# Input projection of a hybrid decoder layer: the first group's P and GB columns as a pair by seven products

## The chip, the cores and the metric

The kernel runs on one core of one Trainium2 chip, as a single launch. The metric is the device time of the launch in microseconds (us). Times of the kernel before are 1523.72, 1524.24 and 1524.89 us in three runs; the median is 1524.24 us. One further execution was profiled; that one took 1524.25 us.

## The reference, cut to what matters

One layer is computed for 256 tokens of width 2048, in float32. Two token mixers share one input projection, whose columns are split into queries, keys, values, a gate z, two small rows, the input of a pooling mixer and two gates:

```python
proj = jnp.einsum('bsd,de->bse', rmsnorm(x, norm_mix_w[l]), w_in[l])
q, k, v, z, b_raw, a_raw, p_in, g_a, g_b = jnp.split(proj, splits, axis=-1)
qkv = jax.nn.silu(causal_dwconv(jnp.concatenate([q, k, v], axis=-1), conv_qkv_w[l]))
...
o = gated_delta_rule(q, k, v, g_log, beta).astype(x.dtype)
y_a = (rmsnorm(o, gdn_norm_w[l]) * jax.nn.silu(z)).reshape(bsz, seq, D_LIN)
pooled = causal_multiscale_pool(p_in.reshape(bsz, seq, N_POOL_GROUPS, POOL_GROUP_DIM))
y_b = jnp.einsum('bsgc,gcd->bsgd', pooled, pool_w[l]).reshape(bsz, seq, D_POOL) * pool_scale[l]
mixed = jax.nn.sigmoid(g_a) * y_a + jax.nn.sigmoid(g_b) * y_b
x = x + jnp.einsum('bsd,df->bsf', mixed, w_out[l])
```

A gated MLP with a causal convolution and a final norm follow. The pooling mixer has four groups of 512 columns, and a group of four heads of the delta rule is as wide; so the kernel works the input projection off in four groups.

## The kernel before, in words

**Tiles and passes.** A weight tile has 256 rows (two blocks of 128) and 512 columns, 512 KB in float32. It is loaded into a buffer `raw` (four in turn), cast by ScalarE (L357) to a rounded float32 `whi`, and VectorE subtracts that from `raw` to get the rest, `wlo` (L368); both have three buffers. The tokens are kept as a high and a low part too. `gemm_a` multiplies a tile with the 256 tokens, in two halves of 128: for each of two blocks and two halves one matmul of high by `whi` (L416), one of low by `whi` (L417), one of high by `wlo` (L418). That makes 12 matmuls of 128x512 for a tile. A block of 2048x512 of the projection is eight tiles, summed in two banks of PSUM, one for each half of the tokens.

**Order of the work.** Group g takes the column blocks K, Q, V, P (the pooling input), GB (the pooling gate), Z, pool and GA, eight tiles each but pool. `srcs` lists the tiles in the order in which they are taken; `weights()` begins the cast and the subtraction of a tile some two tiles ahead. What belongs to the delta rule, the convolutions and the small products is written as a generator (`gdn`, `conv_silu`, `v_conv` and others), of which `side()` runs one piece after each tile. Actions gathered in `later` run when a block's tile number `flush` begins. A scheduler then sets each engine's order of instructions; each engine works its own list strictly in turn.

**Pairs by seven products.** For K and Q of groups 1 to 3, for the output projection and for the MLP, two tiles of each of two column blocks are done together: eight products of a 256x512 tile with half of the tokens (6 matmuls each) become seven, T1, 11, T2, 21, T3, 22 and T4, with sums of weights (`up_sum`, L284, one 128x1024 subtraction each) and sums of tokens. The four tiles, called quads, lie in buffers of their own, each a homes' tag. `pair_product` issues a product and, behind some, puts results together: the result of T1 is copied by ScalarE to `own` in SBUF; that of 11 is copied from one bank into the other (L440); behind T2, VectorE writes `u` = bank + own to SBUF (L443), and at 21 ScalarE copies `u` into the second pair of banks (L432); behind T3, VectorE writes bank + own straight into the second pair (L445). T3 adds to the bank that `u` was read from, so T3's first matmul follows `u`. In the order of K and Q, two items stand between T2 and T3: tile 7 of the block before, and 21.

**What runs in group 0 beside V and P.** The convolutions of K and Q (L931 on ScalarE starts a column block `cy`, then three shifted multiply-adds each on VectorE, L934), the eight exponentials `dec` on ScalarE (L982), whose input row `crow` comes by a DMA and is masked by GpSimd (L974), the eviction of V (`ev`, L876), the value convolution (`vt`, `mv`, L897, L911, L912), then the Gram products (L993, L995) with their diagonals on VectorE (L998). From them a block goes through DRAM to `lb` (`cdd`, L1030, and L1033), and after a wait of so many `side()` calls (`LATE[g]` is part of it) a chain of small VectorE steps on `tb` (L1057 and L1059) inverts 32x32 blocks. The result goes through DRAM again (`tbd`, L1064, to `TT`, L1067), is transposed (L1079), and small matmuls follow (L1103, L1110, then L1121, which reads `U`, copied by ScalarE at L1106, then L1131 and L1139).

Of the kernel before, what the change touches and what calls it, by code (L numbers as in the profile page):

```python
# [28 lines left out]
NR = P // B0  # L29
AHEAD = 2  # L30
WAIT = 5
LATE = (26, 24, 22, 18)
NEVER = -1e30


# [1 line left out]
def kernel(  # L37
# [45 lines left out]
    KQ_FIRST = ("T1", 5, "11", 6, "T2", 7)  # L83
    KQ_MIDDLE = ("21", "T3", "22")
    KQ_THEN = (2, "T4", 3, 4, 5, 6, 7)
    up_w = {("kq", g): [cols(w_in[0], base + 512 * g, KD) for base in (C_K, C_Q)] for g in range(1, 4)}
    srcs = []
    for g in range(4):
        for base in (C_K, C_Q, C_V, C_P, C_GB):
            tiles = cols(w_in[0], base + 512 * g, KD)  # L90
            if g and base == C_K:
                srcs += [("up", ("kq", g), step, 0) if isinstance(step, str) else tiles[step]
                         for step in KQ_MIDDLE + KQ_THEN]
            else:
                srcs += tiles[2:] if g and base == C_Q else tiles
            if g == 0 and base == C_K:
                srcs += [w_in[0, c * 1024 : (c + 1) * 1024, C_B : C_B + P].rearrange("(k p) f -> p k f", p=P)
                         for c in range(2)]
        parts = [cols(pool_w[0, g], 0, 4), cols(w_in[0], C_Z + 512 * g, KD)]
        for part in parts if g == 3 else parts[::-1]:  # L100
            srcs += part
        tiles = cols(w_in[0], C_GA + 512 * g, KD)
        srcs += tiles[:5]
        pair = ("kq", g + 1) if g < 3 else ("out", 0)
        srcs += [("up", pair, step, 0) if isinstance(step, str) else tiles[step] for step in KQ_FIRST]
# [160 lines left out]
    def quad_load(c, n):  # L266

        ch, i = n // 4, (1, 0, 3, 2)[n % 4]
        if c == OUT:
            home = (big if i < 2 else fp).tile([P, 2, 512], F32, tag=OUT_HOMES[i], name=nm("quad"))  # L270
        elif isinstance(c, tuple):
            home = mp.tile([P, 2, 512], F32, tag=KQ_HOMES[i], name=nm("quad"))
        else:
            home = fp.tile([P, 2, 512], F32, tag=UP_HOMES[1 - c % 2][ch][i], name=nm("quad"))
        up_quarters[c, ch, i] = home
        with tc.issue_after(last_load[0]):
            last_load[0] = nc.sync.dma_start(up_quarters[c, ch, i], up_w[c][i % 2][2 * ch + i // 2]).ins
# [105 lines left out]
    def side():  # L383
        next(side_work[0], None)
# [37 lines left out]
    def pair_product(bank, what, tokens, sums):  # L422

        a, b = bank["ps"]
        if what in ("11", "21", "T4"):
            j, t = {"11": (0, 0), "21": (1, 0), "T4": (1, 1)}[what]
            high, low = (lambda kk, f=f: f(2 * j + kk, t) for f in tokens)
        else:
            n = {"T1": 0, "T2": 1, "T3": 2, "22": 3}[what]
            high, low = (lambda kk, s=s: s[:, n, kk * P : (kk + 1) * P] for s in sums)  # L430
        if what == "21":
            nc.scalar.copy(b[:, 0], bank["u"])  # L432
        w = weights()
        ps = {"T1": a[:, 0], "21": a[:, 0], "22": b and b[:, 0]}.get(what, a[:, 1])
        high_first([(ps, high, low)], w, what in ("T1", "11"))
        if what == "T1":
            bank["own"] = cpool.tile([P, 512], F32, tag="sqj", name=nm("own"))
            nc.scalar.copy(bank["own"], a[:, 0])
        elif what == "11":
            nc.scalar.copy(a[:, 0], a[:, 1])  # L440
        elif what == "T2":
            bank["u"] = mp.tile([P, 512], F32, tag="dec0", name=nm("u"))
            nc.vector.tensor_tensor(bank["u"], a[:, 1], bank["own"], op=ALU.add)  # L443
        elif what == "T3":
            nc.vector.tensor_tensor(b[:, 1], a[:, 1], bank["own"], op=ALU.add)  # L445

# [787 lines left out]
    pair_bank = {}  # L1234
    mixing = []

    def kq_steps(steps, ps, flush=3):

        for step in steps:
            if isinstance(step, str):  # L1240
                pair_product(pair_bank, step, (xh, xl), xsums)
            else:
                gemm_a(xh, xl, KD, (step,), ps, flush)

    for g in range(4):
# [27 lines left out]
        if g == 0:  # L1273
# [3 lines left out]
                    fixed_parts()  # L1277

            later.append(after_k)
        e = evict(gemm_a(xh, xl, KD), rsh)  # L1280
        nc.sync.dma_start(vrow[g, SH : SH + S, :].rearrange("(t p) d -> p t d", p=P), e)
        later.append(lambda e=e, g=g, vt2=vt2: v_moved(e, g, vt2))


        win = WINDOWS[g]
        psb = scales(g)
        ps = gemm_a(xh, xl, KD)
        e = evict(ps) if g == 3 else evict(ps, rsh)
        phi = mtile(g, [P, 4, S], F32R, nm("phi"))
        plo = []  # L1290
# [45 lines left out]
                nc.scalar.activation(th[:, t, :], ps[:, t, :], AF.Tanh, scale=rsh[:, t : t + 1])  # L1336
            return th

        tb = gate(gemm_a(xh, xl, KD), "th")
        yb = mp.tile([P, 2, 512], F32, tag="yb", name=nm("yb"))  # L1340
        nc.vector.scalar_tensor_tensor(yb, tb, 1.0, psb.unsqueeze(1).to_broadcast([P, 2, 512]),
                                       op0=ALU.add, op1=ALU.mult)
# [625 lines left out]
```

## Time and profile before

| | |
|---|---|
| median of three runs | 1524.24 us (1523.72 to 1524.89) |
| profiled execution | 1524.25 us, its span 1522.5 us |
| granted TensorE clock | 0.999 |
| first matmul of V, P, GB, Z and GA of group 0 | 60.08, 84.42, 108.82, 134.15, 161.35 us |
| first product of the pair of K and Q of group 1 | 174.95 us |
| DMA | 313.62 MB, mean 206 GB/s |

Times inside the profile count from the start of the span; what lies around the span is the difference of 1.75 us. PE is TensorE's matmuls, PEld its weight loads, DVE is VectorE, ACT is ScalarE, POOL is GpSimd, SP issues most DMAs. In a timeline row stand the start, the length (of a run of like instructions, from the first's start to the last's end), the engine, the line, the operation, what is written and read by tile names, and the shape; a bracket tells of the idle time of the engine before the row and what ended it. Successive instructions of an engine overlap a little, so the step from start to start is shorter than the length.

### The profile page before, as it was taken

Reading aid. Unit: us, or ns where it says so; the run is one execution under the profiler, and the core shown is the slowest. Engines: PE = TensorE matmul, PEld = TensorE weight load, DVE = VectorE, ACT = ScalarE, POOL = GpSimd, SP = SyncE. Lnnn points to the kernel's source line nnn. Section 1 sums busy time; section 2 is a strip of 40 time slices with the busy share of each in tenths; the row PEclk is TensorE's granted clock in tenths of the full one; section 3 lists DMA queues with packets and bytes.
Section 4 is the critical chain, followed back from the end, with each engine's and each line's share of the span. In section 5 each row is a group of like instructions: output and inputs, shape, how many; then the busy total and the mean of one; then the engine's idle time right before and its main releaser. Section 6 shows DMA issues by size and latency. Waiting matters only on the chain.

```text
span 1522.5 us, 20282 instructions
## 1 busy us (share of the span) xinstructions
PE 1513.1 (99%) x7260; PEld 1250.8 (82%) x7260; DVE 1287.0 (85%) x1799; ACT 896.1 (59%) x1160; POOL 75.0 (5%) x97
## 2 busy tenths in 40 slices
PE   9999999999999999999999999999999999999998
PEld 8888888888878888888888888888888888888886
DVE  6779868888688878888777999999998886989896
ACT  7456556455646456456465676667666665555562
POOL 1000001000100001000000000000000011010100
PEclk9999999999999999999999999999999999999999
DMA  8777647784677747774678656666457468566662
GB/s 277 209 226 221 207 139 225 235 255 115 198 221 218 227 127 219 214 238 154 217 227 303 198 164 218 221 212 216 152 164 238 142 212 276 172 223 219 220 220 100
DMA packets 170099, 313.62 MB, mean 206 GB/s; under 512 B 23650, under 2 KB 27010, under 8 KB 169870
## 3 DMA queue, kind: packets, MB, share of 16 engines
q1 hardware_dynamic: 160864, 283.17, 59.0%
q0 software_dynamic: 7344, 27.27, 5.5%
q10 hardware_dynamic: 1790, 1.89, 0.4%
q8 instruction: 57, 0.93, 0.2%
q14 instruction: 44, 0.36, 0.1%
HBM read 303.33 MB, written 8.95 MB: 205 GB/s over the span
## 4 chain that ended last, share of the span: by engine, by line
PE 98%; DVE 1%; issue 1%; ACT 0%; POOL 0%; POOLq 0%; DVEq 0%
PE psg L455 28%; PE psm L418 14%; PE psm L416 14%; PE psm L417 14%; PE psm L1644 8%; PE psg L1644 7%; PE psm L455 4%; PE psm L606 1%; PE psm L1712 1%; PE psg L505 1%; PE psg L993 1%; DVE wlo L368 1%; PE psg L995 0%; PE psm L521 0%; PE psg L1139 0%
## 5 line engine op out<-in xcount | busy, mean ns | idle before, releaser
L357 ACT CAST whi<-raw 128x1024 fp32r<-128x1024 f32 x400 | 419.9, 1052 | 311.0 <-PE psm L417 157.9
L368 DVE TENSOR_TENSOR wlo<-raw,whi 128x1024 fp32r<-128x1024 f32 x398 | 484.1, 1220 | 119.3 <-ACT whi L357 113.9
L357 ACT CAST whi<-quad 128x1024 fp32r<-128x1024 f32 x217 | 227.9, 1053 | 167.5 <-PE psg L455 46.2
L368 DVE TENSOR_TENSOR wlo<-quad,whi 128x1024 fp32r<-128x1024 f32 x217 | 263.4, 1220 | 39.9 <-ACT whi L357 34.8
L416 PE MATMUL psm<-whi,xhl 128*128 128x512 f32 x384 | 150.0, 391 | 0.0
L417 PE MATMUL psm<-whi,xhl 128*128 128x512 f32 x384 | 149.9, 390 | 0.0
L418 PE MATMUL psm<-wlo,xhl 128*128 128x512 f32 x384 | 139.0, 393 | 0.0
L455 PE MATMUL psg<-whi,fhl 128*128 128x512 f32 x504 | 127.1, 389 | 0.0
L284 DVE TENSOR_TENSOR quad<-quad,quad 128x1024 f32<-128x1024 f32 x92 | 111.9, 1217 | 0.1
L455 PEld LDWEIGHTS psg<-whi,fhl 128*128 128x128 f32 x504 | 94.6, 188 | 19.7
L416 PEld LDWEIGHTS psm<-whi,xhl 128*128 128x128 f32 x384 | 72.1, 188 | 15.0
L417 PEld LDWEIGHTS psm<-whi,xhl 128*128 128x128 f32 x384 | 72.1, 188 | 14.9
L418 PEld LDWEIGHTS psm<-wlo,xhl 128*128 128x128 f32 x384 | 71.7, 188 | 14.6
L455 PE MATMUL psg<-wlo,fhl 128*128 128x512 f32 x252 | 69.8, 389 | 0.0
L455 PE MATMUL psg<-whi,ups 128*128 128x512 f32 x216 | 58.1, 391 | 0.0
L455 PEld LDWEIGHTS psg<-wlo,fhl 128*128 128x128 f32 x252 | 47.3, 188 | 9.9
L1644 PE MATMUL psm<-whi,hhi 128*128 128x512 f32 (+1 forms) x140 | 54.2, 387 | 0.0
L1644 PE MATMUL psm<-whi,hlo 128*128 128x512 f32 (+1 forms) x140 | 53.7, 386 | 0.0
L1644 PE MATMUL psm<-wlo,hhi 128*128 128x512 f32 (+1 forms) x140 | 50.2, 386 | 0.0
L455 PEld LDWEIGHTS psg<-whi,ups 128*128 128x128 f32 x216 | 40.3, 188 | 8.5 <-issue 0.2
L1644 PE MATMUL psg<-whi,hhi 128*128 128x512 f32 (+1 forms) x120 | 46.4, 387 | 0.0
L1644 PE MATMUL psg<-whi,hlo 128*128 128x512 f32 (+1 forms) x120 | 46.1, 386 | 0.0
(495 smaller groups left out, 3001.2 us busy)
## 6 DMA issues: line engine op xcount, KB each, us to landing
raw<-in_w_in_dram SPq DMA_DIRECT2D x212, 512.0 KB, 4.5
raw<-in_w_up_dram SPq DMA_DIRECT2D x104, 512.0 KB, 4.7
quad<-in_w_up_dram SPq DMA_DIRECT2D x72, 512.0 KB, 5.3
raw<-in_w_down_dram SPq DMA_DIRECT2D x56, 512.0 KB, 5.1
quad<-in_w_down_dram POOLq DMA_DIRECT2D x32, 512.0 KB, 5.4
raw<-in_w_out_dram SPq DMA_DIRECT2D x24, 512.0 KB, 3.7
mv<-vrow SPq DMA_DIRECT2D x12, 512.0 KB, 4.9
quad<-in_w_in_dram SPq DMA_DIRECT2D x12, 512.0 KB, 6.8
```

Source lines behind the costliest of these rows:

```text
L284: nc.vector.tensor_tensor(out_, plus_, minus_, op=ALU.subtract)
L357: last_cast[0] = nc.scalar.copy(hi, raw).ins
L368: last_split[0] = nc.vector.tensor_tensor(lo, raw, hi.bitcast(F32), op=ALU.subtract).ins
L416: mm(ps[:, t, :], lh(k, t), hi[:, kk, :], start=(k == 0), stop=False, **seeded)
L417: mm(ps[:, t, :], ll(k, t), hi[:, kk, :], start=False, stop=False, **seeded)
L418: mm(ps[:, t, :], lh(k, t), lo[:, kk, :], start=False, stop=(k == nk - 1), **seeded)
L455: last_product[0] = mm(ps, lhs(kk), w[n][:, kk], stop=False, skip_group_check=True, start=(first and n == 0 and kk == 0 and lhs is high)).ins
L505: nc.tensor.transpose(pt[:, ff, t * P : (t + 1) * P], src[:, t, f * P : (f + 1) * P], ident)
L606: mm(ps_k0[:, t, :], part(k, t), w[:, kk, :], start=(k == 0 and w is hi and part is xh), stop=(k == KD - 1 and w is lo))
L993: mm(pg0, kq[:, h, 0, 0:P], kq[:, h, :, :], start=True, stop=True)
L1644: mm(ps[:, cs], lhs(kk), part_[:, kk, cs], start=(first and kk == 0 and n == 0), stop=(last and kk == 1 and n == 2), skip_group_check=shared)
L1712: nc.tensor.transpose(out_[f // 2][:, f % 2, t * P : (t + 1) * P], e[:, t, f * P : (f + 1) * P], ident)
```

## The change

The first two tiles of P and the first two of GB, in group 0, become a pair by seven products: 7 x 6 = 42 matmuls where 8 x 6 = 48 were. The products are not done in a row but set singly among the last tiles of V (T1 behind V's tile 4, then 5, 11, 6, T2, 7, T3) and the tiles of P (21, 2, 22, 3, T4, 4 to 7). GB has only tiles 2 to 7 left, in the banks that the pair has begun. `kq_steps` gets an argument by which `side()` runs after each product. The quads' four buffers are those of `mtile` 1, 2, 5 and 6. The second pair of banks is taken only at 22: `u` and a second sum `u2` (behind T3) are written to SBUF, into the buffers `w1` and `w2`, and ScalarE copies both into the banks then. The wait `LATE` ahead of group 0's `tb` goes from 26 to 19.

```diff
-LATE = (26, 24, 22, 18)
+LATE = (19, 24, 22, 18)
...
+    PG_FIRST = ("T1", 5, "11", 6, "T2", 7, "T3")
+    PG_THEN = ("21", 2, "22", 3, "T4", 4, 5, 6, 7)
+    up_w["pg", 0] = [cols(w_in[0], base, KD) for base in (C_P, C_GB)]
...
+            elif g == 0 and base in (C_V, C_P):
+                srcs += tiles[:5] if base == C_V else []
+                srcs += [("up", ("pg", 0), step, 0) if isinstance(step, str) else tiles[step]
+                         for step in (PG_FIRST if base == C_V else PG_THEN)]
...
-    for pair in (("kq", 1), ("kq", 2), ("kq", 3), ("out", 0)):
+    for pair in (("pg", 0), ("kq", 1), ("kq", 2), ("kq", 3), ("out", 0)):
...
+        elif c == ("pg", 0):
+            home = mtile((1, 2, 5, 6)[i], [P, 2, 512], F32, nm("quad"))
...
-        if what == "21":
+        if what == ("22" if "home" in bank else "21"):
+            if b is None:
+                b = bank["ps"][1] = pm()
+                nc.scalar.copy(b[:, 1], bank["u2"])
             nc.scalar.copy(b[:, 0], bank["u"])
...
-            bank["u"] = mp.tile([P, 512], F32, tag="dec0", name=nm("u"))
+            bank["u"] = mp.tile([P, 512], F32, tag=bank.get("home", ("dec0",))[0], name=nm("u"))
             nc.vector.tensor_tensor(bank["u"], a[:, 1], bank["own"], op=ALU.add)
+        elif what == "T3" and "home" in bank:
+            bank["u2"] = mp.tile([P, 512], F32, tag=bank["home"][1], name=nm("u2"))
+            nc.vector.tensor_tensor(bank["u2"], a[:, 1], bank["own"], op=ALU.add)
...
+            ps = gemm_a(xh, xl, KD, range(5))
+            pair_bank.update(ps=[pm(), None], home=("w1", "w2"))
+            kq_steps(PG_FIRST, ps, 1, True)
...
+            ps = pair_bank["ps"][0]
+            kq_steps(PG_THEN, ps, 2, True)
+            other_ps = pair_bank["ps"][1]
+            pair_bank.clear()
...
-        tb = gate(gemm_a(xh, xl, KD), "th")
+        tb = gate(gemm_a(xh, xl, KD) if g else gemm_a(xh, xl, KD, range(2, 8), other_ps, 2), "th")
```

In the whole program TensorE has 6903 matmuls where it had 6909. VectorE has nine instructions more (four sums, three more `wlo`, `u`, `u2`) and ScalarE seven (three casts, four copies); the counts of SP and GpSimd are the same. The lines move: L357 becomes L366 (cast), L368 L377 (`wlo`), L284 L293 (sum), L416 to L418 become L425 to L427, L455 L470 (a product's matmuls), L443 L455 (`u`), L440 L452 (copy of 11), L931 L946 and L934 L949 (convolution), L982 L997 (`dec`), L1103 L1118, L1110 L1125, L1121 L1136.

**ScalarE around `dec`, at the end of V.** Before, the cast behind the eight exponentials (`whi_975`) is that of P's tile 0:

```order
L357 CAST whi_943<-raw_941 128x1024
...
L931 ACTIVATE cy_812<-psg_802,cqw 128x256
L982 ACTIVATE dec_132_827<-crow_829,ncum 128x128
...
L982 ACTIVATE dec_133_828<-crow_829,ncum 128x128
L357 CAST whi_975<-raw_973 128x1024
L931 ACTIVATE cy_812<-psg_802,cqw 128x256
L931 ACTIVATE cy_812<-psg_807,cqw 128x256
L357 CAST whi_1004<-raw_1002 128x1024
```

Of the change, the first cast here (`whi_972`) is that of V's tile 6, `whi_1003` that of T2, `whi_1020` that of V's tile 7, `whi_1051` that of T3 and `whi_1065` that of 21:

```order
L366 CAST whi_972<-raw_970 128x1024
...
L946 ACTIVATE cy_820<-psg_810,cqw 128x256
L450 COPY own_961<-psm_949 128x512
L997 ACTIVATE dec_136_835<-crow_837,ncum 128x128
...
L997 ACTIVATE dec_137_836<-crow_837,ncum 128x128
L366 CAST whi_1003<-quad_690 128x1024
L946 ACTIVATE cy_820<-psg_810,cqw 128x256
L366 CAST whi_1020<-raw_1018 128x1024
L946 ACTIVATE cy_820<-psg_815,cqw 128x256
L452 COPY psm_949<-psm_950 128x512
L366 CAST whi_1051<-quad_710 128x1024
L366 CAST whi_1065<-quad_762 128x1024
```

The exponentials, which stood ahead of the cast of P's first tile, now stand ahead of that of T2, and V's last tile is cast behind it.

**VectorE at the same place.** Before, from the `wlo` of P's tile 0 to that of P's tile 2 (`wlo_1047`):

```order
L368 TENSOR_TENSOR wlo_977<-raw_973,whi_975 128x1024
L934 SCALAR_TENSOR_TENSOR cy_812<-psg_802,cqw,cy_812 128x255
L934 SCALAR_TENSOR_TENSOR cy_812<-psg_807,cqw,cy_812 128x255
L368 TENSOR_TENSOR wlo_1006<-raw_1002,whi_1004 128x1024
...
L934 SCALAR_TENSOR_TENSOR cy_812<-psg_807,cqw,cy_812 128x253
L368 TENSOR_TENSOR wlo_1047<-raw_1043,whi_1045 128x1024
```

Of the change, from the `wlo` of T2 to that of 21 (`wlo_1067`) and of P's tile 2 (`wlo_1087`); L293 makes the sums for T3 and for T4:

```order
L377 TENSOR_TENSOR wlo_1005<-quad_690,whi_1003 128x1024
L293 TENSOR_TENSOR quad_710<-quad_690,quad_710 128x1024
L949 SCALAR_TENSOR_TENSOR cy_820<-psg_810,cqw,cy_820 128x255
L377 TENSOR_TENSOR wlo_1022<-raw_1018,whi_1020 128x1024
...
L377 TENSOR_TENSOR wlo_1053<-quad_710,whi_1051 128x1024
L293 TENSOR_TENSOR quad_690<-quad_762,quad_690 128x1024
L949 SCALAR_TENSOR_TENSOR cy_820<-psg_815,cqw,cy_820 128x254
L949 SCALAR_TENSOR_TENSOR cy_820<-psg_810,cqw,cy_820 128x253
L455 TENSOR_TENSOR u_1062<-psm_950,own_961 128x512
L377 TENSOR_TENSOR wlo_1067<-quad_762,whi_1065 128x1024
L949 SCALAR_TENSOR_TENSOR cy_820<-psg_815,cqw,cy_820 128x253
L377 TENSOR_TENSOR wlo_1087<-raw_1083,whi_1085 128x1024
```

Between the `wlo` of T2 and `u` stand the `wlo` of V's tile 7 and of T3, two sums and five steps of the convolution.

**TensorE at the end of the group.** Before, the first of the delta rule's small products (L1103) stand behind the pair's product 11 (`wlo_1903`) and inside GA's tile 6 (`wlo_1917`):

```order
L455 MATMUL psm_1900<-wlo_1903,xhl_115 128x512 x2
L1103 MATMUL psg_1646<-T,ga_126_821 32x32 x4
...
L1110 MATMUL psg_1670<-qp_1062,sel 128x32
L418 MATMUL psm_1739<-wlo_1917,xhl_116 128x512
```

Of the change they stand behind the pair's product 22 (`wlo_2017`), inside tile 2 of group 1's K (`whi_2027`):

```order
L470 MATMUL psm_2012<-wlo_2017,xs_784 128x512 x2
L425 MATMUL psm_1918<-whi_2027,xhl1a 128x512
L426 MATMUL psm_1918<-whi_2027,xhl1a 128x512
L1118 MATMUL psg_1599<-T,ga_130_829 32x32 x4
...
L1125 MATMUL psg_1623<-qp_1075,sel 128x32
L425 MATMUL psm_1919<-whi_2027,xhl1a 128x512
L426 MATMUL psm_1919<-whi_2027,xhl1a 128x512
L1136 MATMUL psg_1642<-U_1608,TT 32x32 x8
```

They come later by the rest of GA's tile 6, its tile 7 and four products, and between L1125 and L1136 stand two large matmuls.

More of the change, by code (lines that the diff above doesn't have):

```diff
@@ L93 @@
                          for step in KQ_MIDDLE + KQ_THEN]
+            elif g == 0 and base in (C_V, C_P):
+                srcs += tiles[:5] if base == C_V else []
+                srcs += [("up", ("pg", 0), step, 0) if isinstance(step, str) else tiles[step]
+                         for step in (PG_FIRST if base == C_V else PG_THEN)]
             else:
-                srcs += tiles[2:] if g and base == C_Q else tiles
+                srcs += tiles[2:] if g and base == C_Q or g == 0 and base == C_GB else tiles
             if g == 0 and base == C_K:
@@ L1235, with kq_steps @@
     mixing = []
-    def kq_steps(steps, ps, flush=3):
+    def kq_steps(steps, ps, flush=3, with_side=False):
         for step in steps:
@@ L1241, in kq_steps @@
                 pair_product(pair_bank, step, (xh, xl), xsums)
+                if with_side:
+                    side()
             else:
@@ L1279 @@
             later.append(after_k)
-        e = evict(gemm_a(xh, xl, KD), rsh)
+        if g:
+            ps = gemm_a(xh, xl, KD)
+        else:
+            ps = gemm_a(xh, xl, KD, range(5))
+            pair_bank.update(ps=[pm(), None], home=("w1", "w2"))
+            kq_steps(PG_FIRST, ps, 1, True)
+        e = evict(ps, rsh)
         nc.sync.dma_start(vrow[g, SH : SH + S, :].rearrange("(t p) d -> p t d", p=P), e)
@@ L1286 @@
         psb = scales(g)
-        ps = gemm_a(xh, xl, KD)
+        if g:
+            ps = gemm_a(xh, xl, KD)
+        else:
+            ps = pair_bank["ps"][0]
+            kq_steps(PG_THEN, ps, 2, True)
+            other_ps = pair_bank["ps"][1]
+            pair_bank.clear()
         e = evict(ps) if g == 3 else evict(ps, rsh)
```

## The prediction, blind

> **What bounds the kernel now.** I read the profile page first, for the engine that sets the end: its busy times and its chain of work that ended last.
>
> ```profile
> span 1522.5 us, 20282 instructions
> PE 1513.1 (99%) x7260; PEld 1250.8 (82%) x7260; DVE 1287.0 (85%) x1799; ACT 896.1 (59%) x1160; POOL 75.0 (5%) x97
> PE 98%; DVE 1%; issue 1%; ACT 0%; POOL 0%; POOLq 0%; DVEq 0%
> ```
>
> 98% of the chain is TensorE (PE). The second view is that of TensorE's waits, which says how much of the span isn't matmuls in sequence:
>
> ```profile
> PE psm L521 <- POOL ones L511: 1.1, 1, 1.1
> PE psg L455 <- DVE wlo L368: 0.3, 1, 0.3
> PE psm L418 <- DVE wlo L368: 0.2, 1, 0.2
> ```
>
> These 1.6 us are all, and none lies in the first group's V, P or GB. So a matmul less is worth its cadence, and any wait that the change makes is paid in full. The cadence comes from two stretches of the chain, whose columns are start, length and count:
>
> ```profile
> 839.61 6.80 PE psg L455 x30
> 847.77 23.13 PE psg L455 x102
> ```
>
> 6.80 / 30 and 23.13 / 102 are both 0.2267 us for a 128x512 matmul. The third view is the busy time by stretches of 5 us around the change, columns PE, PEld, DVE, ACT, POOL, granted clock, DMA share, GB/s:
>
> ```profile
> 75.00:80.00 5.00, 5.00 (x28) 4.02 (x27) 2.88 (x6) 1.35 (x4) 0.21 (x1) 1.00 0.68 172
> 80.00:85.00 5.00, 5.00 (x26) 4.14 (x25) 1.11 (x1) 4.54 (x12) 1.01 (x2) 1.00 0.37 143
> 85.00:90.00 5.00, 5.00 (x24) 4.11 (x23) 5.00 (x10) 4.00 (x7) 0.00 (x0) 1.00 0.63 122
> 90.00:95.00 5.00, 5.00 (x24) 4.14 (x23) 4.91 (x7) 2.60 (x4) 0.00 (x0) 1.00 0.79 299
> ```
>
> TensorE never waits here, but VectorE (DVE) goes from 2.88 and 1.11 us of 5 to full between 85 and 95 us. That is where the change sets its pair. The timelines of ScalarE (ACT) and VectorE say why; the columns are start, length, and in brackets the idle time before with what ended it:
>
> ```profile
> 77.07 0.48 ACT L931 ACTIVATE cy<-psg,cqw 128x256 f32<-128x256 f32 x1 [0.30 <-PE psg L505]
> 80.46 2.45 ACT L982 ACTIVATE dec<-crow,ncum 128x128 f32<-128x128 f32 x8 [2.92 <-POOL crow L974]
> 82.82 1.04 ACT L357 CAST whi<-raw 128x1024 fp32r<-128x1024 f32 x1
> 84.48 1.04 ACT L357 CAST whi<-raw 128x1024 fp32r<-128x1024 f32 x1
> ...
> 83.89 1.23 DVE L368 TENSOR_TENSOR wlo<-raw,whi 128x1024 fp32r<-128x1024 f32 x1 [4.80 <-ACT whi L357]
> 85.03 0.87 DVE L934 SCALAR_TENSOR_TENSOR cy<-psg,cqw,cy 128x255 f32<-128x255 f32 x2
> 85.82 1.22 DVE L368 TENSOR_TENSOR wlo<-raw,whi 128x1024 fp32r<-128x1024 f32 x1
> 86.95 1.64 DVE L934 SCALAR_TENSOR_TENSOR cy<-psg,cqw,cy 128x254 f32<-128x254 f32 x4
> ...
> 84.19 0.39 PE L418 MATMUL psm<-wlo,xhl 128*128 128x512 f32 x1
> 84.42 0.39 PE L416 MATMUL psm<-whi,xhl 128*128 128x512 f32 x1
> ```
>
> ScalarE stands until 80.46 at the eight exponentials (dec), which need a row from POOL. So no weight is cast until 82.82, VectorE idles 4.80 us, and then it works off what has gathered. TensorE starts P's first tile at 84.42, with about 1 us in hand.
>
> **The change part by part.** *Matmuls.* Eight tile products of 6 become seven: 6 matmuls less, 6 x 0.2267 = -1.36 us, all on the path.
>
> *Interruptions.* In the changed order TensorE passes from weight matmuls to small ones and back 165 times, before 169, so two interruptions fewer. One costs what it adds beside its own matmuls:
>
> ```profile
> 69.14 0.61 PE L418 MATMUL psm<-wlo,xhl1b 128*128 128x512 f32 x2
> 69.69 0.61 PE L815 MATMUL psg<-mid,glog 128*16 128x128 f32 x4
> 70.23 0.50 PE L416 MATMUL psm<-whi,xhl1b 128*128 128x512 f32 x1
> 70.57 0.40 PE L417 MATMUL psm<-whi,xhl1b 128*128 128x512 f32 x1
> ```
>
> 69.69 is 0.10 later than two cadences after 69.14, and 70.57 is 0.11 later than one after 70.23: 0.2 each, -0.4 us together. Bounds: 0 and -0.4.
>
> *VectorE around V's end.* The change adds nine VectorE instructions, and the order puts the late part of them into the full stretch. ScalarE comes first: its eight dec stand ahead of T2's cast, as ahead of P0's before, and POOL's row is no earlier. So T2's whi is cast from 82.82 to 83.86, V's tile 7 after one more cy (0.41) from about 84.1 to 85.2. TensorE's 48 matmuls up to tile 7 of V are as many as before P0 now, so it would want tile 7 at 84.42: 0.8 us late there. VectorE starts at 83.89 with wlo of T2. In its new order follow the sum for T3, one convolution step (L949 in the new numbering), wlo of tile 7, two steps, wlo of T3, the sum for T4, two steps, and then u (L455 there). From start to start a 128x1024 takes 1.13 to 1.14 us (83.89 to 85.03, 85.82 to 86.95), a step 0.4 (0.87 / 2 and 1.64 / 4). u has a row of its own, from a later group, where L443 makes it:
>
> ```profile
> 186.67 0.69 DVE L443 TENSOR_TENSOR u<-psm,own 128x512 f32<-128x512 f32 x1 [0.20 <-PE psm L455]
> ```
>
> 5 x 1.13 + 5 x 0.41 + 0.69 = 8.4, so u ends at 92.3. T3 must wait for it, because its matmuls add to the bank that u reads. Behind tile 7's start stand 22 matmuls ahead of T3 (12 of tile 7, 6 of T2, the 4 of the 21 with whi): 84.42 + 22 x 0.2267 = 89.41. So TensorE waits 2.9 us, the 0.8 at tile 7 contained. Behind u come wlo of 21 (1.13), a step (0.41) and wlo of P2 (1.13), to 95.0; TensorE has 10 matmuls from T3 to P2's first wlo and arrives at 92.3 + 2.27 = 94.6: 0.4 more. wlo for 22 is ready at 95.0 + 1.13 (vt) + 0.69 (u2) + 1.13 = 97.95, where TensorE gets 18 matmuls later at 99.1: no wait. Sum +3.3 us; 2 if the steps come when VectorE has idled less, 4.5 if each semaphore adds some tenths. What else stands behind the waiting matmul on TensorE's queue is tiles of P; who waits for them is the conv and V's eviction, both with time.
>
> The Trainium skill ("VectorE: DVE Perf Modes", section on the TRN2 errata) says that a VectorE operation pays a fixed extra latency each time, exposed between instructions, and gives (N+151)/0.96 ns for an fp32 add, 1.224 us for 1024. The row's duration agrees with that (1.22 and 1.23), its spacing from start to start doesn't (1.13 to 1.14). By the page's figure the chain to u would end 5 x 0.09 = 0.45 later and the forecast would be 0.45 us higher.
>
> *ScalarE, SP and POOL.* Seven more ScalarE instructions, three casts and four copies, fall where it is busy for 12.5 of 20 us (75 to 95); what they delay is in the walk above. SP's count stays: four loads of P and GB tiles become loads of quads, where the DMA share is 0.37 to 0.79. Nothing, unless a load is late; then what the next tile lacks, up to 1 us. POOL's list doesn't change.
>
> *Side work comes later.* The conv's end, the grams and all that follows them move about three tiles back in the program; only the wait ahead of tb is cut, by 7 calls. The first place where that could tell is lb, which goes through DRAM:
>
> ```profile
> 121.81 3.67 SPq L1030 DMA_DIRECT2D cdd<-ga  x8
> 126.63 2.20 SPq L1033 DMA_DIRECT2D lb<-cdd  x4
> 133.95 0.19 DVE L1057 TENSOR_TENSOR tmp<-lb,tb 128x31 f32<-128x31 f32 x1
> 142.31 0.39 PE L416 MATMUL psm<-whi,xhl1b 128*128 128x512 f32 x1
> ```
>
> Before, from the first cdd to VectorE's first use of lb were 12.1 us. In the new order the second half's grams stand in GB's tile 5 instead of 2, some 6 to 8 us later, so lb is there at about 140 to 142, and its first use stands ahead of wlo of Z's tile 3. TensorE wants that wlo at 143.2, four matmuls after the tile's start at 142.31. VectorE will wait, TensorE just not: 0, and up to 1.
>
> *End of the group.* The chain of tb, which ended at 171.4 behind tile 4 of GA, now ends behind wlo of GA's tile 7, and its way through DRAM follows:
>
> ```profile
> 171.19 0.17 DVE L1059 TENSOR_TENSOR tb<-tb,tmp 128x8 f32<-128x8 f32 x1
> 171.39 2.61 SPq L1064 DMA_DIRECT2D tbd<-tb  x4
> 175.38 1.82 SPq L1067 DMA_DIRECT2D TT<-tbd  x4
> DMA to landing us min/median/max: 1.9/1.9/1.9
> 182.63 1.22 DVE L368 TENSOR_TENSOR wlo<-raw,whi 128x1024 fp32r<-128x1024 f32 x1
> 184.19 0.40 PE L416 MATMUL psm<-whi,xhl 128*128 128x512 f32 x1
> 182.14 1.10 ACT L1106 COPY U<-psg 32x128 f32<-32x128 f32 x4
> ```
>
> The fourth TT issues at 176.8 and lands 1.9 later, 7.3 after tb's end. Tile 7's wlo (182.63) ends 0.4 us ahead of the tile's first matmul (184.19); with the last tb step behind it tb ends 0.2 ahead. In the new order 38 matmuls, 8.6 us, lie from there to the first small product (L1118). The transposes and the addition between them end about 8.4 after tb, at 8.2: in time by 0.4. The product behind it (L1136) needs U, four copies of 1.10 us together, and only L1125 and two matmuls stand between: it comes 0.5 us too soon. Before, 18 large matmuls lay there. +0.5; bounds 0 and 2.8 (below).
>
> Sum: -1.36 - 0.4 + 3.3 + 0.5 = +2.0. The profiled execution took 1524.25 us (1522.5 of span and 1.75 around it), the median of three is 1524.24, so the base is the same: 1524.2 + 2.0 = 1526.3 us.
>
> **The rivals.** *A: the waits are hidden.* It does what seven products for eight can do: -1.36 - 0.4, 1522.5 us. For it speaks that pairs of the same kind run later with hardly a wait while VectorE is nearly full:
>
> ```profile
> 180.00:190.00 10.00, 10.00 (x103) 7.93 (x102) 8.78 (x16) 6.15 (x11) 0.00 (x0) 1.00 0.40 119
> 190.00:200.00 10.00, 10.00 (x66) 7.97 (x66) 9.81 (x14) 6.38 (x10) 0.00 (x0) 1.00 0.19 54
> ```
>
> Against it: there two items stand between T2 and T3, and VectorE idles just before u (0.20 in its row); here one tile does, and VectorE has a backlog. It comes true if u is issued by about 89 us, that is, if dec is over some 3 us sooner because POOL's row comes sooner.
>
> The Trainium skill ("Perfetto Trace Analysis", Identifying the Most-Contended Engine) says that the engine to improve first is the most occupied one, judged by stretch where regimes differ, and that TensorE's busy share is no measure of it. For 85 to 95 us the page would name VectorE (9.91 of 10), and so speaks against adding work to it to save matmuls; TensorE's chain of 98% says the opposite for the whole. By that rule alone VectorE's added late work (sums of T3 and T4, u, 2.95 us) would be paid, less what TensorE saves: 1524.2 + 2.95 - 1.76 = 1525.4, within the forecast's own range.
>
> *B: slower by more than the bound.* The tb chain is late at the group's end. It decides as soon as tb ends 0.2 us after TensorE starts tile 7 of GA: from there each tenth is a wait at L1118. tb stands behind wlo of tile 7, which TensorE needs only ten matmuls into the tile, 2.27 us later. If it comes that late, the wait is 2.27 + 0.2 + 8.4 - 8.6 = 2.3 us: 1528.6. For it: VectorE at 8.78 of 10 there, a long chain of dependent little steps, and lb late at its start; against it: tile 7's wlo was early before.
>
> That the matmuls aren't saved can be left out: the order has 6903 where 6909 stood.
>
> **How the numbers follow.** Forecast 0.55 (1526.3, its own range 1524.5 to 1527.8), A 0.25, B 0.20. The range for all reaches from A less half a microsecond to B and a little: 1522.0 to 1529.0. A measurement of this kernel can tell about 0.2%, 3.05 us: faster is below 1521.2, slower above 1527.3. A lies in the middle band but for 0.03; of the forecast 0.07 lies above; B is above. Faster 0.03, same 0.70, slower 0.27.
>
> **What would show it.** Right: TensorE's waits list T3's matmul (L470) on VectorE's u (L455) with about 2 to 3 us near 90 us; tile 7 of V on ScalarE's cast under 1 us; dec still at about 80.5; 0.5 us at L1136. Wrong: no such wait (A), dec much earlier, or the wait at L1118 on the transposes (B). A time under 1521 would mean that something besides these matmuls had been on the path.

## The result, and the profile after

The changed kernel takes 1541.49 us (median of four runs, 1540.60 to 1543.92), the kernel before 1524.03 us beside it (four runs, 1523.72 to 1524.89). The ratio is 1.0117, interval 1.0104 to 1.0129: 17.5 us slower. The forecast was 1526.3 us, its range ended at 1529.0.

The page of the changed kernel, its span, busy times and the engines' shares of the chain:

```profile
span 1540.2 us, 20284 instructions
...
PE 1519.1 (99%) x7254; PEld 1251.7 (81%) x7254; DVE 1293.3 (84%) x1808; ACT 901.7 (59%) x1167; POOL 70.6 (5%) x97
...
PE 86%; DVE 3%; DMA 2%; issue 1%; SPq 0%; ACT 0%; POOL 0%; POOLq 0%; DVEq 0%
```

TensorE is still busy for 99%, and yet its busy time grew by 6 us with six matmuls fewer: part of the loss is slower matmuls. The waits of TensorE, with sum, count and longest:

```profile
PE psg L1118 <- DVE T L1094: 6.4, 2, 5.2
PE psm L427 <- DVE wlo L377: 3.5, 8, 0.6
PE psm L470 <- DVE u L455: 1.4, 1, 1.4
PE psm L536 <- POOL ones L526: 1.1, 1, 1.1
PE psg L520 <- DVE sz L1432: 0.6, 1, 0.6
PE psg L470 <- DVE wlo L377: 0.3, 1, 0.3
```

13.3 us where 1.6 stood. The forecast wait on `u` is there and half as long; the greatest is on the transposes ahead of the delta rule's small products (L1118), once in group 0 and once, with 5.2 us, elsewhere. To see where, the large weight matmuls of two traces are counted from the end of the program, where both have the same ones, and the starts of the same matmul are subtracted. This gives how late a kernel runs at a place, and the places are ones by which all kernels have done the same small products. The columns are kernels, the last two of them experiments told below:

| place, by its time in the trace of before | forecast, running sum | changed kernel | V's multiplications 3 splits later | pair also set earlier |
|---|---|---|---|---|
| 134.2, Z of group 0 starts | +1.5 | +1.7 | +0.9 | -0.5 |
| 250, group 1 | +2.0 | +5.6 | +5.1 | +0.2 |
| 345, group 1 | +2.0 | +5.8 | +5.2 | +0.2 |
| 527, group 2 | +2.0 | +7.3 | +4.7 | +0.3 |
| 697, group 3 | +2.0 | +10.2 | +4.7 | +0.3 |
| 749, behind group 3's small products | +2.0 | +18.0 | +4.7 | +0.3 |
| 1400, the MLP | +2.0 | +17.8 | +4.4 | 0.0 |

V, P and GB of group 0, where the change is, cost in sum about what was forecast. Only 5.6 us are lost by 250, and 12 more fall in groups 1 to 3, whose code the change doesn't touch. First the place of the change, ScalarE, VectorE and TensorE there (a bracket is the idle time ahead and what ended it):

```profile
79.84 2.45 ACT L997 ACTIVATE dec<-crow,ncum 128x128 f32<-128x128 f32 x8 [1.88 <-POOL crow L989]
...
90.90 0.68 DVE L455 TENSOR_TENSOR u<-psm,own 128x512 f32<-128x512 f32 x1
...
91.63 1.20 PE L470 MATMUL psm<-whi,xs 128*128 128x512 f32 x4 [1.37 <-DVE u L455]
```

`dec` is at 79.84 (before 80.46), `u` ends at 91.6 (forecast 92.3), T3 waits 1.4 us. VectorE has no idle time left there:

```profile
85.00:90.00 5.00, 4.98 (x22) 3.61 (x20) 5.00 (x7) 3.81 (x5) 0.00 (x0) 1.00 0.33 83
90.00:95.00 5.00, 3.54 (x15) 2.42 (x14) 5.00 (x8) 3.04 (x5) 0.00 (x0) 1.00 0.34 128
95.00:100.00 5.00, 4.92 (x22) 3.72 (x21) 5.00 (x7) 3.33 (x5) 0.00 (x0) 1.00 0.93 320
```

The rest of what VectorE owes then comes later: the Gram products of group 0 begin at 108.9 instead of 97.8, and the chain of `tb` ends at 185.5 instead of 171.4. VectorE, SP and TensorE at the end of group 0:

```profile
185.32 0.17 DVE L1074 TENSOR_TENSOR tb<-tb,tmp 128x8 f32<-128x8 f32 x1
185.85 2.62 SPq L1079 DMA_DIRECT2D tbd<-tb  x4
191.47 1.82 SPq L1082 DMA_DIRECT2D TT<-tbd  x4
193.26 1.45 DVE L1094 STREAM_TRANSPOSE T<-TT 32x256 f32<-32x256 f32 x3 [1.78 <-DMA TT<-tbd]
194.86 0.69 PE L1118 MATMUL psg<-T,ga 32*32 32x32 f32 x32 [1.24 <-DVE T L1094]
198.07 0.63 PE L425 MATMUL psm<-whi,xhl1a 128*128 128x512 f32 x1
198.49 0.63 PE L426 MATMUL psm<-whi,xhl1a 128*128 128x512 f32 x1
```

TensorE waits 1.24 us, and a little behind it the matmuls start 0.42 us apart instead of 0.23; the granted clock of 195 to 200 is 0.75. The chain of work that ended last has the two landings, start and length:

```profile
187.86 3.46 DMA tbd<-tb
...
192.35 1.91 DMA TT<-tbd
```

The first took 3.5 us where 1.9 was counted on.

In group 2, VectorE of the kernel before:

```profile
441.18 0.29 DVE L998 CUSTOM_DVE_ANT_0 jk<-psg,ident 128x128 f32<-128x128 f32 x1
...
443.28 0.48 DVE L1012 SCALAR_TENSOR_TENSOR ga<-psg,sj,dec 128x256 f32<-128x256 f32 x1
...
445.47 1.23 DVE L911 TENSOR_TENSOR mv<-mv,taps 128x1024 f32<-128x1024 f32 x1 [0.54 <-DMA mv<-vrow]
```

and of the changed one:

```profile
447.71 0.29 DVE L1013 CUSTOM_DVE_ANT_0 jk<-psg,ident 128x128 f32<-128x128 f32 x1
...
453.21 1.23 DVE L926 TENSOR_TENSOR mv<-mv,taps 128x1024 f32<-128x1024 f32 x1 [5.20 <-DMA mv<-vrow]
454.36 0.28 DVE L1013 CUSTOM_DVE_ANT_0 jk<-psg,ident 128x128 f32<-128x128 f32 x1
...
466.41 0.48 DVE L1027 SCALAR_TENSOR_TENSOR ga<-psg,sj,dec 128x256 f32<-128x256 f32 x1
```

This is the core of the case. Before, the Gram diagonals `jk` and the result `ga` came first and V's multiplication `mv` after them, when its row had nearly landed (0.54 us of waiting). Now half of the diagonals stand behind `mv`. VectorE stands 5.20 us for a DMA, with work in its list that could have run (the Gram products of that half had ended by 448.9), and `ga` is 23 us later, of which the kernel's own lateness there is 5 to 7. The list of VectorE's waits says that it happens three times:

```profile
DVE mv L926 <- DMA mv<-vrow: 13.3, 3, 5.2
```

3.5, 5.2 and 4.7 us in groups 1, 2 and 3; before, four waits came to 1.3 us together. The bill is paid at the end of group 3. VectorE, SP and TensorE of the changed kernel:

```profile
715.49 0.17 DVE L1074 TENSOR_TENSOR tb<-tb,tmp 128x8 f32<-128x8 f32 x1
715.69 2.53 SPq L1079 DMA_DIRECT2D tbd<-tb  x4
718.28 0.61 PE L470 MATMUL psm<-wlo,mhi 128*128 128x512 f32 x2
719.59 1.82 SPq L1082 DMA_DIRECT2D TT<-tbd  x4
722.65 1.83 DVE L1094 STREAM_TRANSPOSE T<-TT 32x256 f32<-32x256 f32 x4 [0.73 <-DMA TT<-tbd]
724.07 1.06 PE L1118 MATMUL psg<-T,ga 32*32 32x32 f32 x32 [5.18 <-DVE T L1094]
726.09 0.63 PE L426 MATMUL psm<-whi,xhl 128*128 128x512 f32 x1
726.51 0.63 PE L427 MATMUL psm<-wlo,xhl 128*128 128x512 f32 x1
```

`tb` ends at 715.7 (before 686.6), and its way through DRAM and the transposes is not over when TensorE has nothing else to do. The stretches behind it show the clock (last but two):

```profile
715.00:720.00 5.00, 3.90 (x18) 2.88 (x16) 3.37 (x5) 3.48 (x5) 0.00 (x0) 1.00 0.51 134
720.00:725.00 5.00, 0.93 (x32) 0.93 (x32) 3.67 (x6) 0.26 (x2) 0.00 (x0) 0.81 0.77 218
725.00:730.00 5.00, 5.00 (x19) 3.97 (x15) 0.65 (x4) 0.78 (x4) 0.00 (x0) 0.51 0.02 8
730.00:735.00 5.00, 5.00 (x52) 3.91 (x51) 3.37 (x7) 2.21 (x3) 0.00 (x0) 1.00 0.00 2
```

After the wait of 5.18 us the granted clock is 0.51 until about 730: from 725.51 ten matmuls take 4.4 us where ten cadences are 2.27. The wait, these 2.1 us and half a microsecond at the small products make the 7.8 us between 697 and 749 in the table. The Trainium skill ("TensorE: Matmul & The Clock Gate", What's actually happening) says that the clock falls to half after an idle window of about 3.4 us and comes back after as long a busy one. The trace agrees with that here. At 194.86, where one wait of 1.24 us is followed by matmuls 0.42 us apart, the lower clock does not follow from the wait alone: in the run with `LATE` back at 26, told below, a wait of 1.5 us at the same place left the clock at 1.00. Whether the small 32x32 products count as idle, no run here shows.

### The profile page after: what moved, and what is told of

Same layout as the page of the kernel before. It is cut to its first block, busy times and chain, and to the rows that moved or that the text cites. A ratio compares the mean times of both kernels' runs of the same rounds, so it can differ in the third digit from the quotient of the medians.

```text
span 1540.2 us, 20284 instructions
## 1 busy us (share of the span) xinstructions
PE 1519.1 (99%) x7254; PEld 1251.7 (81%) x7254; DVE 1293.3 (84%) x1808; ACT 901.7 (59%) x1167; POOL 70.6 (5%) x97
## 4 chain that ended last, share of the span: by engine, by line
PE 86%; DVE 3%; DMA 2%; issue 1%; SPq 0%; ACT 0%; POOL 0%; POOLq 0%; DVEq 0%
PE psg L470 28%; PE psm L427 12%; PE psm L425 12%; PE psm L426 11%; PE psm L1673 7%; PE psg L1673 7%; PE psm L470 3%; DVE wlo L377 1%; PE psm L1741 1%; PE psg L520 1%; PE psg L1008 1%; DMA tbd<-tb 0%; DMA TT<-tbd 0%; PE psg L1010 0%; DVE quad L293 0%
## 5 line engine op out<-in xcount | busy, mean ns | idle before, releaser
L366 ACT CAST whi<-raw 128x1024 fp32r<-128x1024 f32 x396 | 415.9, 1052 | 326.9 <-PE psm L426 162.2
L377 DVE TENSOR_TENSOR wlo<-raw,whi 128x1024 fp32r<-128x1024 f32 x394 | 479.6, 1221 | 112.0 <-ACT whi L366 101.6
L366 ACT CAST whi<-quad 128x1024 fp32r<-128x1024 f32 x224 | 235.3, 1053 | 175.2 <-PE psg L470 45.9
L377 DVE TENSOR_TENSOR wlo<-quad,whi 128x1024 fp32r<-128x1024 f32 x224 | 272.2, 1221 | 50.2 <-ACT whi L366 45.0
L426 PE MATMUL psm<-whi,xhl 128*128 128x512 f32 x368 | 145.4, 395 | 0.0
L425 PE MATMUL psm<-whi,xhl 128*128 128x512 f32 x368 | 144.9, 394 | 0.0
L427 PE MATMUL psm<-wlo,xhl 128*128 128x512 f32 x368 | 135.5, 396 | 0.9 <-DVE wlo L377 0.9
L470 PE MATMUL psg<-whi,fhl 128*128 128x512 f32 x504 | 126.9, 389 | 0.0
L293 DVE TENSOR_TENSOR quad<-quad,quad 128x1024 f32<-128x1024 f32 x96 | 117.0, 1219 | 0.1
L470 PEld LDWEIGHTS psg<-whi,fhl 128*128 128x128 f32 x504 | 94.6, 188 | 19.7
L427 PEld LDWEIGHTS psm<-wlo,xhl 128*128 128x128 f32 x368 | 69.2, 189 | 16.7 <-DVE wlo L377 2.5
L426 PEld LDWEIGHTS psm<-whi,xhl 128*128 128x128 f32 x368 | 69.7, 189 | 15.1 <-issue 0.7
L425 PEld LDWEIGHTS psm<-whi,xhl 128*128 128x128 f32 x368 | 69.7, 189 | 14.8 <-ACT whi L366 0.4
L470 PE MATMUL psg<-wlo,fhl 128*128 128x512 f32 x252 | 69.8, 389 | 0.0
L470 PE MATMUL psg<-whi,ups 128*128 128x512 f32 x216 | 58.0, 390 | 0.0
L470 PEld LDWEIGHTS psg<-wlo,fhl 128*128 128x128 f32 x252 | 47.3, 188 | 9.8
L470 PEld LDWEIGHTS psg<-whi,ups 128*128 128x128 f32 x216 | 40.3, 188 | 8.5 <-issue 0.3
```

Source lines behind the costliest of these rows:

```text
L293: nc.vector.tensor_tensor(out_, plus_, minus_, op=ALU.subtract)
L366: last_cast[0] = nc.scalar.copy(hi, raw).ins
L377: last_split[0] = nc.vector.tensor_tensor(lo, raw, hi.bitcast(F32), op=ALU.subtract).ins
L425: mm(ps[:, t, :], lh(k, t), hi[:, kk, :], start=(k == 0), stop=False, **seeded)
L426: mm(ps[:, t, :], ll(k, t), hi[:, kk, :], start=False, stop=False, **seeded)
L427: mm(ps[:, t, :], lh(k, t), lo[:, kk, :], start=False, stop=(k == nk - 1), **seeded)
```

## The experiments

Theory A: VectorE's list is full beside V's end and P; what the change adds pushes all later side work back, and the loss in groups 1 to 3 comes from that lateness alone, without the pair having anything to do with it otherwise. Its rivals are the cut of `LATE`, the lateness of `tb` at group 0's end by itself, and the pair's own waits and interruptions on TensorE.

**Only VectorE's work, no pair.** Four additions on a spare buffer, as long as the change's sums, in the kernel before:

```diff
+        with tc.issue_after(last_split[0]):
+            nc.vector.tensor_tensor(spare[0], spare[0], spare[0], op=ALU.add)
...
-        e = evict(gemm_a(xh, xl, KD), rsh)
+        e = evict(gemm_a(xh, xl, KD, extra=() if g else (6, 7)), rsh)
...
-        ps = gemm_a(xh, xl, KD)
+        ps = gemm_a(xh, xl, KD, extra=() if g else (0, 1))
```

> The kernel before, with no pair, and four spare 128x1024 additions on VectorE beside V's tiles 6 and 7 and P's tiles 0 and 1 of group 0 (4.5 us of work that nothing reads). Theory A (lateness is carried on: what is put on the full VectorE there pushes convolution, Gram products and the inversion back, each group hands the delay to the next through the four PSUM banks of the small products, and TensorE pays where the groups end and at the end of group 3): the order of this kernel already shows groups 2 and 3 as late as in the changed one, so +10 to +18 us, with a wait of several us at L1103 in group 3. Theory B (the price is the pair's own: u, its copies, its borrowed buffers): 0 to +2 us, and no wait at L1103.

Measured 1539.57 us, ratio 1.0101 (1.0084 to 1.0118): +15.5 us, without a pair. TensorE's waits and the first of VectorE's on `mv`, with lines two higher than before:

```profile
PE psg L1105 <- DVE T L1081: 5.3, 1, 5.3
PE psm L418 <- DVE wlo L368: 4.6, 9, 1.1
```

```profile
DVE mv L913 <- DMA mv<-vrow: 13.1, 3, 4.8
```

The same picture as the changed kernel's: 5.3 us ahead of the small products of group 3, 13.1 us of VectorE behind V's loads. So neither the pair, nor its waits, nor `LATE` is needed for the loss.

**Only `tb` late.** In the kernel before, the wait ahead of group 0's `tb` is lengthened:

```diff
-LATE = (26, 24, 22, 18)
+LATE = (35, 24, 22, 18)
```

> The kernel before, with LATE of group 0 at 35 instead of 26: only the start of the tb chain of group 0 is put off by nine side calls, about 12 us. Theory A: a wait for T or U at the end of group 0 and some delay in group 1, +3 to +7 us; the order shows groups 2 and 3 at their old places, so nothing from them and no long wait in group 3. Theory B: 0 to +1 us.

Measured 1527.08 us, ratio 1.0019 (1.0009 to 1.0028): +3.0. `tb` ends at 190.4, later than in the changed kernel. The first Gram products of groups 1 and 2 in this run:

```profile
284.35 1.02 PE L993 MATMUL psg<-kq 128*128 128x512 f32 x2
...
440.07 1.02 PE L993 MATMUL psg<-kq 128*128 128x512 f32 x2
```

Group 1's Grams are 24.8 us later than before (259.57), but group 2's only 1.7 (438.39). In group 1 `mv` comes to stand ahead of the Gram products here too, and VectorE waits 4.6 us for it; in group 2 the order is back. So the lateness of `tb` alone passes into group 1 and ends there, and one group in that order does not make the loss. What makes groups 2 and 3 late too must be something else.

**The cut of `LATE` undone.** In the changed kernel:

```diff
-LATE = (19, 24, 22, 18)
+LATE = (26, 24, 22, 18)
```

> The changed kernel with LATE of group 0 back at 26. If the cut to 19 matters, the tb chain starts up to 9 us later and the time grows by 2 us or more; theory A with lb as the limit (the first tb step waits for lb's landing at 142, and not for the count of calls): the same time as the changed kernel within 1.5 us. Theory B: the same too.

Measured 1543.61 us, ratio 1.0127 (1.0112 to 1.0142), an interval that overlaps that of the changed kernel: the cut of `LATE` did no harm. The first step on `tb` is at 143.2 instead of 142.5, because it waits for `lb` either way. A correction to the text above: `side()` runs twice for a tile, once after each block of 128 rows, so the cut of seven calls is three and a half tiles, not seven.

**The pair's sums on GpSimd.** In the changed kernel, the four sums of weights leave VectorE:

```diff
-                nc.vector.tensor_tensor(out_, plus_, minus_, op=ALU.subtract)
+                eng = nc.gpsimd if c == ("pg", 0) else nc.vector
+                eng.tensor_tensor(out_, plus_, minus_, op=ALU.subtract)
```

> The changed kernel with the pair's four sums of weights made by GpSimd instead of VectorE (4.5 us less for VectorE). Theory A: the Gram products come a tile earlier in group 0, but groups 1 to 3 stand in the order as late as before, so only the wait at the end of group 0 shrinks: 2 to 4 us less than the changed kernel, about 1538. Theory B: the wait for u shrinks to nothing, 1 to 2 us less. If GpSimd takes 3 us or more for a sum, the products wait for it instead and nothing is won.

Measured 1539.99 us, ratio 1.0101 (1.0086 to 1.0116): 1.5 us below the changed kernel in the median, with intervals that overlap, and the Gram products of groups 2 and 3 stand among the large matmuls at the same late places. The wait ahead of the small products of group 3 stays (lines one higher):

```profile
PE psg L1119 <- DVE T L1095: 5.3, 1, 5.3
```

Theory A in its simple form, so much VectorE work, so much loss, does not fit: 4 x 1.13 us less work brought 1.5 in the median. A sum took 2.40 us on GpSimd. What all these losing runs share is VectorE standing at `mv` in groups 1 to 3. So the theory took its second form: lateness changes the order in VectorE's list. In groups 1 to 3 `kq` is finished a tile or more later, V's multiplications are pinned to a weight split, and so `mv`, waiting for its DMA, comes to stand ahead of the Gram diagonals. In the order of the changed kernel this can be read: in groups 2 and 3 `kq` ends in V's tile 7 instead of 6, the second half's Gram products stand in P's tile 6 instead of 1.

**V's multiplications later.** One number in the changed kernel, the pin in groups 1 to 3:

```diff
-            with tc.issue_after(splits[splits_of[g] + n + (3 if g == 0 else 0)]):
+            with tc.issue_after(splits[splits_of[g] + n + (3 if g == 0 else 3)]):
```

> The changed kernel with one number altered: the three multiplications of V's shifted copies (L926, which wait for mv's DMA) stand three weight splits later on VectorE in groups 1 to 3. Theory A in its second form (lateness is amplified there: in the changed kernel the Gram products come one tile late, VectorE then reaches the multiplication first and stands 5.2 us for its DMA with the Gram diagonals behind it, and the delta rule loses some 20 us in each group): the order shows groups 2 and 3 back at the places of before, so 9 to 12 us less than the changed kernel, 1529 to 1533, with no long wait at L1118 in group 3. Theory A in its first form (lateness alone is handed on through the PSUM banks, whatever VectorE waits for): at most 3 us less.

Measured 1529.09 us, ratio 1.0032 (1.0021 to 1.0044) against 1523.79 for the kernel before: 5.3 us are lost where 17.5 were, so some 12 are back. TensorE's two longest waits:

```profile
PE psg L1118 <- DVE T L1094: 1.6, 1, 1.6
PE psm L470 <- DVE u L455: 1.3, 1, 1.3
```

L1118 waits in group 0 alone now, VectorE's waits for `mv` are down to one of 0.3 us, and `ga` of group 2 is at 446.30 instead of 466.41. In the table the lateness stays at about 5 from group 1 on. This shows the second form: the order behind `mv` costs 12 us, and 5 remain without it.

**The same with one split.** As above, with 1 in place of the last 3.

> The same with one split instead of three. The order shows group 3 back at its old places and group 2 in between. Second form: the 7.8 us lost in group 3 come back, and about 1 of the 2.9 of group 2: 1531 to 1535. First form: at most 1.5 us less than the changed kernel.

Measured 1529.64 us, ratio 1.0038 (1.0023 to 1.0053): nearly all of it already, more than expected. VectorE still stands twice, `mv` <- DMA 5.5 us in sum, but TensorE's wait of 5.2 us at the small products of group 3 is gone (1.4 us, in group 0).

**The control.** The same number in the kernel before.

> The kernel before with the same later multiplications, as a control: its Gram products already stand ahead of them. The order is nearly that of before. Both forms: within 1 us of before.

Measured 1523.89 us, ratio 1.0000 (0.9990 to 1.0009). The later pin is worth nothing by itself; it only heals. One of its ten executions took 8769.07 us; it is not in the ratio, and what caused it is open.

**The pair earlier.** The pair among V's tiles 2 to 7, with V's multiplications 3 splits later in groups 1 to 3 and 2 later in group 0 (5 in place of 3):

```diff
-    PG_FIRST = ("T1", 5, "11", 6, "T2", 7, "T3")
-    PG_THEN = ("21", 2, "22", 3, "T4", 4, 5, 6, 7)
+    PG_FIRST = ("T1", 2, "11", 3, "T2", 4, "T3", 5, "21", 6, 7)
+    PG_THEN = (2, "22", 3, "T4", 4, 5, 6, 7)
...
-                srcs += tiles[:5] if base == C_V else []
+                srcs += tiles[:2] if base == C_V else []
...
-            with tc.issue_after(splits[splits_of[g] + n + (3 if g == 0 else 0)]):
+            with tc.issue_after(splits[splits_of[g] + n + (5 if g == 0 else 3)]):
...
-            ps = gemm_a(xh, xl, KD, range(5))
+            ps = gemm_a(xh, xl, KD, range(2))
```

> The pair set from V's tile 2 on, where VectorE is half idle (T1, 2, 11, 3, T2, 4, T3, 5, 21, 6, 7 beside V, then 2, 22, 3, T4 beside P), V's multiplications two splits later in group 0 and three in groups 1 to 3. The order shows the Gram products of groups 1 to 3 at most two tiles off those of before, and the small products at the end of group 0 two pair products later. Second form: no long wait in groups 1 to 3, the wait for u gone, 1 to 3 us left at the end of group 0: 1522 to 1527. First form: 1530 or more, since convolution and Gram products of group 0 are still later than before.

Measured 1524.36 us, ratio 1.0004 (0.9995 to 1.0014): the time of the kernel before, 4.7 us below the run with the pin alone. TensorE's waits:

```profile
PE psm L536 <- POOL ones L526: 1.1, 1, 1.1
PE psm L427 <- DVE wlo L377: 0.6, 3, 0.2
PE psg L470 <- DVE wlo L377: 0.3, 1, 0.3
```

No wait on `u`, none at L1118. The Gram products of group 0 begin at 101.2, `tb` ends at 178.8. Six matmuls less (1.36 us) leave 0.5 us at Z, since short waits came: the matmuls at 86.64 and 95.65 start 0.05 us behind the end of a `wlo`, and the one at 94.39 as closely behind that of a cast. They are 0.1 to 0.4 us late, and the matmul behind each is late by another 0.11. By group 1 the half microsecond is gone.

**How much added work it takes.** The kernel before with one spare addition (behind V's tile 7), with two (also behind P's tile 0), and with four and the later pin:

```diff
-        e = evict(gemm_a(xh, xl, KD), rsh)
+        e = evict(gemm_a(xh, xl, KD, extra=() if g else (7,)), rsh)
```

> The kernel before with one spare addition on VectorE (1.13 us) behind V's tile 7 in group 0. Second form of theory A has a threshold: the order leaves the Gram products of groups 1 to 3 where they were, so 0 to +0.7 us. If lateness were simply handed on, a quarter of what four additions cost: about +4 us.

Measured 1525.64 us, ratio 1.0013 (1.0004 to 1.0023): +2.0 for 1.13 us of work, more than expected, with no wait ahead of the small products. VectorE waits for `mv` five times already, 4.8 us in sum, but these waits cost nothing: counted as in the table, this trace is 1.5 us late at Z of group 0, where TensorE has waited 1.0 us for `wlo`, and no later behind it.

```diff
-        e = evict(gemm_a(xh, xl, KD), rsh)
+        e = evict(gemm_a(xh, xl, KD, extra=() if g else (7,)), rsh)
...
-        ps = gemm_a(xh, xl, KD)
+        ps = gemm_a(xh, xl, KD, extra=() if g else (0,))
```

> The same with two spare additions (2.3 us), behind V's tile 7 and P's tile 0. Second form: the order shows the Gram products of groups 2 and 3 behind V's multiplications, just as with four, so +9 to +16 us, with a wait of about 5 us at L1103 in group 3 (line numbers of before, moved by the added lines). Handed on in proportion: about +8 us, and half of the wait.

Measured 1538.33 us, ratio 1.0095 (1.0081 to 1.0109): +14.7. TensorE's wait on the transposes and VectorE in group 2:

```profile
PE psg L1105 <- DVE T L1081: 5.3, 1, 5.3
```

```profile
451.86 1.23 DVE L913 TENSOR_TENSOR mv<-mv,taps 128x1024 f32<-128x1024 f32 x1 [5.74 <-DMA mv<-vrow]
```

Counted as in the table, this trace is only 0.7 us late at 250 and 15.0 at 749. One addition costs 2.0 us, two 14.7 and four 15.5: a threshold, not a price for each. That moving four sums to GpSimd brought so little fits it.

```diff
-            with tc.issue_after(splits[splits_of[g] + n + (3 if g == 0 else 0)]):
+            with tc.issue_after(splits[splits_of[g] + n + 3]):
```

> Four spare additions, and V's multiplications three splits later in groups 1 to 3. Second form: groups 2 and 3 stand in the order as before, so what four additions cost in groups 1 to 3 (12 of 15 us) goes away: +1 to +4 us. In proportion: +10 us or more.

Four additions and the later pin: 1526.42 us, ratio 1.0019 (1.0010 to 1.0028), +2.8. 12.7 of the 15.5 us that these additions cost are gone with one number, without a pair in the program. L1105 is in TensorE's list no more.

**The early pair with its sums on GpSimd.** Both edits from above together.

> The early pair (from V's tile 2 on, V's multiplications moved) with its four sums of weights made by GpSimd. The order has the small products at the end of group 0 back at the place of before, so of the six matmuls' 1.36 us something should be left: 1522.0 to 1523.8, which would beat both kernels. If a sum on GpSimd takes so long that T2, T3 or T4 wait for it, 1524 to 1527.

Measured 1525.80 us, ratio 1.0013 (1.0004 to 1.0022): in the median 1.4 us worse than with the sums on VectorE, with intervals of the ratios that overlap. A GpSimd sum here:

```profile
69.70 3.25 POOL L293 TENSOR_TENSOR quad<-quad,quad 128x1024 f32<-128x1024 f32 x1 [3.24 <-DVE wlo L377]
```

3.25 us where VectorE takes 1.22, and TensorE waits 1.0 us for ScalarE's casts. 1.6 us of the loss are there by Z's start. No version here beats the kernel before.

## Why the prediction was wrong, point by point

- **Matmuls, -1.36:** right; six fewer.
- **Interruptions, -0.4:** not found. The six places between 60 and 136 us where small products stand among the large ones cost the same in both traces, so up to Z nothing was saved; whether it was behind Z, the runs don't separate.
- **The wait on `u` and P2, +3.3:** right in its mechanism and near in its sum, not in its parts: 2.9 us. `u` ended at 91.6, and T3 started 1.5 us late. Four more waits are too short for the list, but each of these matmuls starts 0.05 us behind the end of what it needs: V's tile 7 at 84.60 behind its cast (0.12 late, 0.8 forecast) and at 87.20 behind its `wlo` (0.19), P2 at 94.28 behind its `wlo` (0.25), and one at 96.02 behind `u2` (0.25), a wait that the prediction did not have. Behind each of the five the next matmul is 0.11 late, which the sum did not have either. At Z the kernel was 1.7 us late where 1.5 was forecast; that this agrees so well is in part luck, as the smaller waits offset the interruptions that were not saved.
- **End of group 0, +0.5:** mis-sized, measured +3.9. The wait fell on L1118 itself, as rival B had it, not on L1136. The way from the end of `tb` to the transposes was taken from before; there the landings took 1.9 us. Here that of `tbd` took 3.5, so the first transposes began 7.8 us after `tb` where 5.8 stood, and the half clock behind the wait, which no term had, came on top. In the run with `LATE` at 26, where the wait was 1.5 us and the clock did not fall there, this place cost 2.7.
- **Side work later, "0, and up to 1":** this is the step that failed. The prediction followed the late Gram products to the next two places that need them, `lb` and the end of group 0, and stopped there. It did not look at what a later `kq` and later Grams do to the order in VectorE's list in groups 1 to 3, where no line of code was changed. There `mv` came to stand ahead of the diagonals, VectorE stood 13.3 us for DMAs, and 12 us were lost, 7.8 of them at one place: a wait of 5.18 us and the half clock behind it.
- **Rival B** gave the right sign and, with 1528.6 us, about what the run with the later pin takes (1529.1). Its mechanism is there in group 0, but that the size agrees is in part luck: it had the wait at L1118 at 2.3 us, where 1.2 to 1.6 were measured, and no half clock behind it. It left out group 3, where the same wait is four times as long, since TensorE has work for only 3 us after that group's `tb`.
- **The Trainium skill's rule** on the most occupied engine ("Perfetto Trace Analysis", Identifying the Most-Contended Engine) spoke against the change, and the time agrees in sign. The price that the prediction worked out by it, +1.2 us, does not: VectorE's work was paid as lateness and a changed order.

Shown are the loss by added VectorE work alone, its threshold, and that V's multiplications standing ahead of the Gram work make 12 of the 17.5 us, since one number gives as much back in the changed kernel and in one that has added VectorE work but no pair. Only argued is how the lateness passes from group 0 to the `kq` of group 1: through the in-order lists and the four small PSUM banks that the groups share, of which no run took one away. The five microseconds that stay with the later pin lie up to group 1's start: 0.9 by Z, the wait on `u` in it, and some 4 at the end of group 0, where the wait at L1118 is 1.6 and the clock of 195 to 200 is 0.70. They are not divided further.

## What to carry to other kernels

When a change makes an engine's side work later, follow the lateness through every stage that has the same in-order list, to the last one, and look above all for an instruction there that waits for a DMA and is pinned to a place: work that was ahead of it can come to stand behind it. Before adding work to an engine that is full in a stretch, add spare work of the same length to the old kernel there; two additions of 1.13 us would have told here what the change does. And a wait of TensorE is dearer than its length when the clock falls behind it.

## What the runs showed of the hardware that was not expected

- A wait of 5.18 us was followed by ten matmuls at 0.43 us instead of 0.227, a granted clock of 0.51. Behind a wait of only 1.24 us, with 32x32 products after it, matmuls stood 0.42 us apart as well, and the clock of that stretch was 0.75; in the run with `LATE` at 26 a wait of 1.5 us at the same place left it at 1.00.
- Behind each of five waits of 0.12 to 1.5 us, the matmul after the one that had waited started 0.11 us late as well.
- A 128x1024 float32 subtraction took 2.40 to 3.25 us on GpSimd and 1.22 on VectorE.
- The landing of the same small store `tbd` took 3.46, 2.10 and 1.96 us at three places of the changed kernel's chain.
